# A DiT block's later modulation: four contraction tiles of 256 columns at a time in place of two of 512

## The chip, the cores and the metric

One core of a Trainium2 chip runs the whole block. The metric is the device time of one execution in microseconds (us). TensorE (PE) has a granted clock of 1.2 or 2.4 GHz; the profile gives it as a share of the higher one.

## The reference

A diffusion-transformer block: 1024 latent tokens and 256 context tokens of width 1024. From the conditioning vector c come six modulation rows, each 1024 long: shift, scale and gate of the mixer and of the experts.

```python
mod_l = (jax.nn.silu(c) @ w_ada[l] + b_ada[l])[:, None, :]
sh1_l, sc1_l, gt1_l, sh2_l, sc2_l, gt2_l = jnp.split(mod_l, 6, axis=-1)
u_c, u_l = hybrid_mixer(modulate(ctx, sh1_c, sc1_c), modulate(x, sh1_l, sc1_l), ...)
x = post_norm(DEEP_ALPHA * x + gt1_l * u_l, ln_g[l, 0], ln_b[l, 0])
f_l = hierarchical_moe(modulate(x, sh2_l, sc2_l).reshape(B * L, D), *moe_args)
x = post_norm(DEEP_ALPHA * x + gt2_l * f_l, ln_g[l, 1], ln_b[l, 1])
```

The mixer projects all tokens, runs a gated delta rule (four heads, two directions, with a triangular solve for each chunk of 64) and a gated linear recurrence, and projects back. The experts are 32 in four groups; each token goes to two.

## The kernel before

The work stands in stages, one after the other in time: the first two modulation rows, the layer norm and the transposition of the tokens (to about 85 us); the projections with everything that hangs on them (85 to some 556 us); the scan over chunks with the output projection, norms and router (to 850 us); the experts and the last norm (to the end).

The change is in the second stage. `proj_cm` (lines 407 to 414) loads 128 columns of `w_in` into a tile `wraw`, splits it into a high and a low part (`split_w`, lines 388 to 400: the high part on ScalarE or VectorE at line 398, the low part mostly on GpSimd at line 399), and runs three matmuls of each contraction tile (`mm3`, lines 402 to 405) into a PSUM tile `pj`. `head(h)` projects k, v and q of a head and convolves them (`conv`, line 434 on VectorE). `prep_a` makes decays, transposes (line 508) and products of the chunks (line 587); `prep_b` solves the triangular systems on VectorE, 31 steps of a product and a subtraction (lines 619 and 621). GpSimd works at `prep_a`'s masks (lines 518 and 552 to 557).

The other four modulation rows, 4096 channels, are computed in the gaps of that stage by `ada_late` (lines 688 to 715). It takes 512 channels at a time (loop over n, eight turns). For each, four loads on the SP queue (line 694) bring two contraction tiles of 128 rows by 512 columns each into `wraw`, a tag of three buffers that it shares with the loads of `w_in`. After each load stand two float32 matmuls (line 701): the stationary operand `cT[:, k, :]` is 32 columns wide, and the result goes to partitions 32g to 32g+31 of `pr`, with g = k % 4, so that it uses one strip of 32 columns of the array. The first four tiles open the four strips, the last four add to them. Then ScalarE copies `pr` (line 703), four matmuls of line 707 (eight records) sum the strips into four columns of a `pm` tile, and VectorE adds the bias (line 709). At the end the rows go to DRAM (line 715).

The tiles `pm` and `pj` have four PSUM buffers each (`PA['PM']`). `ada_late` is a generator: `next(side, None)` is called once after each piece of a head (lines 828 to 838), and each load and each copy ends in a yield. So the program's text sets only a priority. The order of the instructions on each engine is drawn up by the framework from its own estimates of durations (line 1649):

```python
with _tile.TileContext(nc, schedule_with_timeline_sim=True) as tc:
```

Engines then work their queues in order.

Of the kernel before, what the change touches and what calls it, by code (L numbers as in the profile page):

```python
# [9 lines left out]
F32 = mybir.dt.float32  # L10
# [8 lines left out]
P = 128  # L19
# [62 lines left out]
PA = {'ORD': 'x0 z1 x1 g0 z2 z0 x2 x3 g1 g2 g3 z3', 'ZB': 'qvsa', 'ADV1': 1, 'ADV2': 2, 'PER': 1, 'A0': 0, 'SQB': 1, 'GELU': 0, 'GSTG': 1, 'PM': (4, 4), 'HIV': (3, 8, 10, 14, 17, 20, 23), 'LOV': (2, 4, 21), 'C1V': (0, 1, 3, 4, 5, 14, 15, 19, 23), 'PSS': 0, 'TOK': (('kt', 4), ('v', 4)), 'EMV': 0, 'RGV': 0, 'CVB': 3, 'WRB': 3, 'HO': 'kvq', 'SQP': 0, 'YMA': 0}  # L82
# [5 lines left out]
def hybrid_block(ctx, tc, x, c, ctx_in, c_ctx, w_ada, b_ada, w_in, conv_qkv_w, dn_a_log, dn_dt_bias, dn_onorm_w,  # L88
         rg_conv_w, rg_conv_b, rg_wa, rg_ba, rg_wi, rg_bi, rg_lambda, w_out, ln_g, ln_b,
         router_wg, router_bg, router_we, router_be, w_e_gate, w_e_up, w_e_down, ranks, only, out):  # L90
    nc = tc.nc
# [20 lines left out]
    def pm():  # L112
        return psx[1].tile([P, 512], F32, name="pm", tag="pm", bufs=psx[2])

    def pj():
        return psx[1].tile([P, 512], F32, name="pj", tag="pj", bufs=psx[3])
# [65 lines left out]
    def later(s, after):  # L182

        tc.add_manual_dep(s.ins, after.ins.name, mybir.DependencyInfo(mybir.DependencyClass.Sync, mybir.DependencyReason.SCHED_ONLY), reason="needed sooner")
        return s
# [4 lines left out]
    cT = ca.tile([P, KT, 32], F32, name="cT")  # L190
# [3 lines left out]
    w_ada_v = w_ada[0].rearrange("(k p) n -> p k n", p=P)  # L194
# [71 lines left out]
    for gi, (tiles, t0) in enumerate((((8, 9), 1024), ((0, 1, 2, 3), 0), ((4, 5, 6, 7), 512))):  # L266
        nt = len(tiles)
        N = nt * P
        s = 0 if t0 < 1024 else 1
        pbd = pj()  # L270
        for k in range(KT):
# [10 lines left out]
            g = k % 4  # L282
# [94 lines left out]
    wp = wps.enter_context(tc.tile_pool(name="wp", bufs=1, side="right"))  # L377
# [310 lines left out]
    def ada_late():  # L688

        for n in range(8):  # L690
            pr = pj()
            for q in range(4):
                w = wp.tile([P, 2, 512], F32, name="wraw", tag="wraw", bufs=PA["WRB"])
                s = nc.sync.dma_start(w, w_ada_v[:, 2 * q:2 * q + 2, 2048 + n * 512:2560 + n * 512])
                if len(ada) < ADAN:
                    ada.append(later(s, lastx))
                yield
                for i in range(2):
                    k = 2 * q + i
                    g = k % 4  # L700
                    nc.tensor.matmul(pr[32 * g:32 * g + 32, :], cT[:, k, :], w[:, i, :], start=k < 4, stop=k >= 4)
            r = wp.tile([P, 512], F32, name="cv", tag="cv", bufs=PA["CVB"])
            nc.scalar.copy(r, pr)
            yield
            p1 = pm()
            for i in range(4):
                nc.tensor.matmul(p1[:, i:i + 1], r[:, i * P:(i + 1) * P], sel32[:, 0:1], start=True, stop=True)
            c0 = 4 * n
            nc.vector.tensor_tensor(mcol[:, c0:c0 + 4], p1[:, 0:4], bc_[:, 16 + c0:20 + c0], op=ALU.add)

        p1 = pm()
        nc.tensor.transpose(p1[0:32, 0:P], mcol, ident)
        r = wp.tile([P, 512], F32, name="cv", tag="cv", bufs=PA["CVB"])
        nc.scalar.copy(r[0:32, 0:P], p1[0:32, 0:P])
        nc.sync.dma_start(md[0].rearrange("(k p) -> k p", p=P), r[0:32, 0:P])
# [103 lines left out]
    def z_gate(h):  # L819
# [6 lines left out]
        nc.sync.dma_start(zd[:, h, :], zT)  # L826

    side = ada_late()
    rest_ = [dict(x=rg, z=z_gate, g=rg_out)[c_[0]](int(c_[1])) for c_ in PA["ORD"].split()]
    nu_ = 0  # L830
# [92 lines left out]
    w = {}  # L923
# [669 lines left out]
    for t0 in range(0, 8, 2):  # L1593
# [21 lines left out]
        for t in ts:  # L1615
# [6 lines left out]
            for b in range(2):  # L1622
                c0 = 64 * (t if (t + b) % 2 == 0 else 15 - t)
# [30 lines left out]
```

## Time and profile before

| what | value |
|---|---|
| median of three runs | 1289.57 us (1284.93 to 1298.79) |
| the profiled execution | 1280.62 us |
| its span, first to last instruction | 1278.9 us |
| mean granted clock of PE | 0.925 |
| PE busy | 1112.5 us (87%) |
| DVE busy | 682.3 us (53%) |
| ACT busy | 422.4 us (33%) |
| POOL busy | 424.9 us (33%) |

Engines: PE is TensorE's matmuls, PEld its weight loads, DVE VectorE, ACT ScalarE, POOL GpSimd, SP the queue that issues most DMAs. A busy time is the union of an engine's records; a matmul's record includes its way through the array, so records of neighbouring matmuls overlap, and the time that a matmul holds PE is read from start to start. A float32 matmul leaves two records. Names such as `pj<-wraw,cT` are out<-in by the program's tiles; `128*32 128x512` is 128 rows and 32 columns of the array, and 128 partitions by 512 elements of the moving operand. What stands in square brackets is the idle time of the engine before the instruction, and what ended it.

### The profile page before, as it was taken

The page shows a single profiled execution, that of the slowest core. Times are in us where ns is not written, and L with a number is a line of the kernel's source. Part 1 is how long each engine was busy: PE and PEld are TensorE (multiplying, and loading weights), DVE is VectorE, ACT ScalarE, POOL GpSimd, SP SyncE. Part 2 cuts the span into 40 slices and gives each one's busy share as a digit, 9 for nine tenths or more (in the row PEclk, how much of TensorE's full clock was granted, in tenths as well). Part 3 has the DMA queues.
Part 4 walks back from the last instruction along what each step waited for, and adds up shares of the span by engine and source line. Part 5 has one row for each costly group of instructions (what it writes and reads, how often), then busy time and mean ns, then how long its engine had stood idle before and what let it go on. Part 6 is the DMA issues. An engine that isn't in the chain of part 4 may idle for free.

```text
span 1278.9 us, 18429 instructions
## 1 busy us (share of the span) xinstructions
PE 1112.5 (87%) x6810; PEld 701.4 (55%) x6810; DVE 682.3 (53%) x1570; ACT 422.4 (33%) x755; POOL 424.9 (33%) x492
## 2 busy tenths in 40 slices
PE   4799998998999989987999999984898999999720
PEld 1357775776767677665667777772323433443210
DVE  3737479487684975875446766654211322222227
ACT  0535324233321727971222446540211212112003
POOL 1511414232242223353640176841211322222225
PEclk8799999999897999996999999975999999999975
DMA  9413453645536231009886255349999999999955
GB/s 335 163 49 93 140 149 94 189 139 140 141 111 160 69 104 37 17 19 306 266 256 214 93 188 185 114 186 332 336 332 355 342 309 307 308 311 315 314 178 169
DMA packets 208883, 251.43 MB, mean 197 GB/s; under 512 B 37276, under 2 KB 164440, under 8 KB 208792
## 3 DMA queue, kind: packets, MB, share of 16 engines
q1 hardware_dynamic: 194128, 215.94, 53.0%
q0 software_dynamic: 7888, 16.80, 5.7%
q10 hardware_dynamic: 6776, 17.50, 3.5%
q8 instruction: 54, 0.88, 0.3%
q14 instruction: 37, 0.30, 0.1%
HBM read 206.39 MB, written 55.20 MB: 205 GB/s over the span
## 4 chain that ended last, share of the span: by engine, by line
PE 39%; DMA 29%; DVE 17%; issue 6%; POOL 3%; SPq 3%; ACT 3%; DVEq 0%; POOLq 0%; ACTq 0%
DMA w<-in_w_e_up_dram 8%; DMA acc<-y,tbri 5%; PE pj L403 4%; PE pj L405 4%; PE pj L404 4%; DMA acc<-y,rows_to 4%; DMA d<-in_w_e_down_dram 4%; DVE s L621 4%; DVE s L619 4%; DMA wada<-in_w_ada_dram 2%; PE pu L1471 2%; PE p L1148 2%; PE pf L403 2%; PE pf L405 2%; PE pf L404 2%
## 5 line engine op out<-in xcount | busy, mean ns | idle before, releaser
L1471 PE MATMUL pu<-w,xT 128*32 128x512 f32 (+2 forms) x848 | 189.1, 614 | 19.0 <-DMA w<-in_w_e_up_dram 17.0
L403 PE MATMUL pj<-hhi,whi 128*128 128x512 f32 (+1 forms) x480 | 188.6, 393 | 4.5 <-ACT s L439 2.8
L404 PE MATMUL pj<-hlo,whi 128*128 128x512 f32 (+1 forms) x480 | 185.9, 387 | 0.0
L405 PE MATMUL pj<-hhi,wlo 128*128 128x512 f32 (+1 forms) x480 | 184.3, 385 | 0.0
L1471 PEld LDWEIGHTS pu<-w,xT 128*32 128x32 f32 (+2 forms) x848 | 61.8, 135 | 116.9 <-issue 104.0
L403 PEld LDWEIGHTS pj<-hhi,whi 128*128 128x128 f32 x480 | 92.5, 193 | 49.6 <-issue 18.6
L399 POOL TENSOR_TENSOR wlo<-wraw,whi 128x1024 fp32r<-128x1024 f32 x21 | 52.8, 2513 | 155.2 <-ACT whi L398 87.3
L405 PEld LDWEIGHTS pj<-hhi,wlo 128*128 128x128 f32 x480 | 92.7, 193 | 20.8 <-issue 5.7
L1492 PE MATMUL py<-d,hT 128*32 128x512 f32 (+2 forms) x424 | 101.0, 598 | 3.1 <-DMA d<-in_w_e_down_dram 2.1
L404 PEld LDWEIGHTS pj<-hlo,whi 128*128 128x128 f32 x480 | 92.8, 193 | 19.3 <-issue 5.3
L1474 DVE TENSOR_TENSOR hid<-hid,pu 128x256 f32<-128x256 f32 x24 | 10.0, 421 | 138.0 <-ACT hid L1473 138.0
L1496 POOL DMA_INDIRECT acc<-y,rows_to x28 | 41.3, 1476 | 116.4 <-DMA acc<-y,rows_to 51.0
L619 DVE TENSOR_TENSOR s<-s,s 80x31 f32<-80x31 f32 (+15 forms) x124 | 65.4, 527 | 14.4 <-DMA s<-ad 11.8
L434 DVE SCALAR_TENSOR_TENSOR cv<-pj,par,cv 128x504 f32<-128x504 f32 (+3 forms) x96 | 63.9, 668 | 11.3 <-ACT cv L422 10.3
L1493 DVE SCALAR_TENSOR_TENSOR y<-py,tbw,gt 128x512 f32<-128x512 f32 x48 | 35.7, 750 | 62.9 <-PE py L1492 52.8
L1462 ACT ACTIVATE xT<-pf,mod 128x128 f32<-128x128 f32 x96 | 37.8, 455 | 89.4 <-PE pf L1458 82.8
L1464 DVE TENSOR_SCALAR xT<-pf,mod 128x128 f32<-128x128 f32 x96 | 34.8, 405 | 59.4 <-ACT xT L1462 50.2
L1449 POOL DMA_INDIRECT xg<-h2d,tbri x24 | 25.4, 1060 | 117.4 <-PE pf L1458 69.8
L1492 PEld LDWEIGHTS py<-d,hT 128*32 128x32 f32 (+2 forms) x424 | 31.7, 131 | 57.3 <-issue 51.5
L621 DVE TENSOR_TENSOR s<-s,s 80x31 f32<-80x31 f32 (+15 forms) x124 | 61.9, 499 | 2.3
L1473 ACT ACTIVATE hid<-pu 128x256 f32<-128x256 f32 x24 | 9.1, 384 | 147.0 <-PE pu L1471 147.0
L403 PE MATMUL pf<-whi,yh 128*128 128x512 f32 x128 | 53.9, 421 | 1.9 <-DVE x L974 1.2
(483 smaller groups left out, 2123.1 us busy)
## 6 DMA issues: line engine op xcount, KB each, us to landing
w<-in_w_e_gate_dram SPq DMA_DIRECT2D x32, 1024.0 KB, 7.9
w<-in_w_e_up_dram SPq DMA_DIRECT2D x32, 1024.0 KB, 8.3
d<-in_w_e_down_dram SPq DMA_DIRECT2D x32, 1024.0 KB, 6.4
st<-sp SPq DMA_DIRECT2D x52, 384.0 KB, 5.2
wraw<-in_w_ada_dram SPq DMA_DIRECT2D x32, 512.0 KB, 4.6
wraw<-in_w_in_dram SPq DMA_DIRECT2D x24, 512.0 KB, 5.3
wada<-in_w_ada_dram SPq DMA_DIRECT2D x4, 2048.0 KB, 8.4
sp<-t SPq DMA_DIRECT2D x12, 512.0 KB, 4.6
```

Of the source, the lines that this page charges most:

```text
L399: (nc.vector if i in PA["LOV"] else nc.gpsimd).tensor_tensor(lo, raw, hi.bitcast(F32), op=ALU.subtract)
L403: nc.tensor.matmul(o, lh, rh, start=start, stop=False)
L404: nc.tensor.matmul(o, lh, rl, start=False, stop=False)
L405: nc.tensor.matmul(o, ll, rh, start=False, stop=stop)
L434: nc.vector.scalar_tensor_tensor(yo, xi, w(j), yo, op0=ALU.mult, op1=ALU.add)
L619: nc.vector.tensor_tensor(t_, sa[:, j + 1:32, j:j + 1].to_broadcast([80, n, j + 1]), T[:, j:j + 1, 0:j + 1].to_broadcast([80, n, j + 1]), ...
L621: nc.vector.tensor_tensor(T[:, j + 1:32, 0:j + 1], T[:, j + 1:32, 0:j + 1], t_, op=ALU.subtract)
L1462: nc.scalar.activation(self.xT[:, i, 0:u], pt[:, k * P:k * P + u], AF.Identity, bias=mod2[:, 0, i:i + 1], scale=mod2[:, 1, i:i + 1])
L1471: nc.tensor.matmul(pu[o:o + n, :], self.xT[:, k, o:o + n], ws[r][:, k, :], start=k == 0, stop=k == KT - 1)
L1492: nc.tensor.matmul(py[o:o + n, :], self.hT[:, f, o:o + n], ws[r][:, f, qs], start=f == 0, stop=f == 1)
L1493: nc.vector.scalar_tensor_tensor(y[0:u, qs], py[0:u, :], self.weights[0:u], gt2[0:u, qs], op0=ALU.mult, op1=ALU.mult)
L1496: nc.gpsimd.indirect_dma_start(out=acc, out_offset=bass.IndirectOffsetOnAxis(ap=to[0:o + n], axis=0), in_=y[0:o + n], in_offset=None, boun ...
```

## The change

A load brings four contraction tiles of 256 channels in place of two of 512, and its four matmuls go to four strips of the array, 256 columns each. Loads, their bytes, buffers and yields keep their number. The two halves of the channels follow each other: contraction tiles 0 to 3 and 4 to 7 of the first 256 channels, then of the second.

```diff
             for q in range(4):
-                w = wp.tile([P, 2, 512], F32, name="wraw", tag="wraw", bufs=PA["WRB"])
-                s = nc.sync.dma_start(w, w_ada_v[:, 2 * q:2 * q + 2, 2048 + n * 512:2560 + n * 512])
+
+                a, c0 = q % 2, q // 2 * 256
+                w = wp.tile([P, 4, 256], F32, name="wraw", tag="wraw", bufs=PA["WRB"])
+                s = nc.sync.dma_start(w, w_ada_v[:, 4 * a:4 * a + 4, 2048 + n * 512 + c0:2304 + n * 512 + c0])
                 if len(ada) < ADAN:
                     ada.append(later(s, lastx))
                 yield
-                for i in range(2):
-                    k = 2 * q + i
-                    g = k % 4
-                    nc.tensor.matmul(pr[32 * g:32 * g + 32, :], cT[:, k, :], w[:, i, :], start=k < 4, stop=k >= 4)
+                for g in range(4):
+                    nc.tensor.matmul(pr[32 * g:32 * g + 32, c0:c0 + 256], cT[:, 4 * a + g, :], w[:, g, :], start=a == 0, stop=a == 1)
```

## Rows read from the trace of the kernel before

**Rows 1.** The page, busy tenths in 40 slices of 32 us
```profile
PE   4799998998999989987999999984898999999720
```

**Rows 2.** Windows: length, busy us (x instructions), granted clock, DMA share, GB/s
```profile
core 0: us, PE busy (x) PEld busy (x) DVE busy (x) ACT busy (x) POOL busy (x), PEclk, DMA share, GB/s
219.00:225.00 6.00, 4.82 (x12) 2.17 (x12) 4.41 (x15) 4.19 (x6) 0.00 (x0) 0.50 0.27 65
85.00:420.00 335.00, 322.51 (x2188) 240.48 (x2187) 226.87 (x548) 112.85 (x178) 101.17 (x71) 0.94 0.49 136
```

**Rows 3.** Chain of waits from 85 to 420 us, shares by line
```profile
by line: PE pj L403 12.5%; PE pj L405 11.7%; PE pj L404 11.5%; DVE s L619 10.4%; DVE s L621 9.7%; PE pj L701 5.8%; DVE cv L434 5.3%; PE pm L587 3.9%; PE pm L658 2.8%; DMA wraw<-in_w_in_dram 2.6%; PE pm L643 2.1%; PE pm L497 1.9%; PE pm L508
```

**Rows 4.** The later modulation, line 701: durations ns min/median/max, first and last start us
```profile
L701 PE MATMUL pj<-wraw,cT x128: 592/617/1063, 89.1 to 417.0; 128*32 128x512 f32 x128
```

**Rows 5.** Windows of line 701 alone: PE and PEld busy us
```profile
85.00:420.00 335.00, 37.24 (x128) 4.98 (x128) 0.94 0.49 136
```

**Rows 6.** Timeline of PE, one load's two tiles: start us, us
```profile
126.12 1.05 PE L701 MATMUL pj<-wraw,cT 128*32 128x512 f32 x4
127.10 0.50 PE L403 MATMUL pj<-hhi,whi 128*128 128x512 f32 x1
```

**Rows 7.** Timeline of PE, two loads' four tiles together, and the projection behind
```profile
133.91 1.06 PE L701 MATMUL pj<-wraw,cT 128*32 128x512 f32 x8
134.91 0.39 PE L403 MATMUL pj<-hhi,whi 128*128 128x256 f32 x1
...
135.49 0.40 PE L404 MATMUL pj<-hlo,whi 128*128 128x512 f32 x1
135.72 0.28 PE L405 MATMUL pj<-hhi,wlo 128*128 128x256 f32 x1
135.84 0.27 PE L403 MATMUL pj<-hhi,whi 128*128 128x256 f32 x1
```

**Rows 8.** Timeline of PE, one load at the lower clock
```profile
222.50 1.92 PE L701 MATMUL pj<-wraw,cT 128*32 128x512 f32 x4
224.36 0.58 PE L403 MATMUL pj<-hhi,whi 128*128 128x256 f32 x1
```

**Rows 9.** Timeline of PEld, weight loads of four tiles
```profile
133.91 0.16 PEld L701 LDWEIGHTS pj<-wraw,cT 128*32 128x32 f32 x8 [0.36 <-issue]
```

**Rows 10.** Timeline of PE, a load's two tiles cut apart
```profile
342.35 1.04 PE L701 MATMUL pj<-wraw,cT 128*32 128x512 f32 x2
343.33 0.44 PE L508 MATMUL pm<-ident,kT 128*128 128x128 f32 x2
343.70 1.05 PE L701 MATMUL pj<-wraw,cT 128*32 128x512 f32 x2
```

**Rows 11.** The page, DMA issues: KB each, median us to landing
```profile
wraw<-in_w_ada_dram SPq DMA_DIRECT2D x32, 512.0 KB, 4.6
wraw<-in_w_in_dram SPq DMA_DIRECT2D x24, 512.0 KB, 5.3
```

**Rows 12.** Line 701, what ended its waits: us, times
```profile
  DMA wraw<-in_w_ada_dram: 0.4, 1
```

**Rows 13.** Timeline of DVE in a triangular solve
```profile
207.22 0.37 DVE L619 TENSOR_TENSOR s<-s,s 80x207 f32<-80x207 f32 x1
207.62 1.35 DVE L621 TENSOR_TENSOR s<-s,s 80x207 f32<-80x207 f32 x1
...
213.32 2.36 DVE L621 TENSOR_TENSOR s<-s,s 80x175 f32<-80x175 f32 x1
...
219.98 0.15 DVE L709 TENSOR_TENSOR mcol<-pm,bc__93 128x4 f32<-128x4 f32 x1
```

**Rows 14.** Timeline of POOL beside it, first and last of seven
```profile
207.48 1.26 POOL L554 TENSOR_TENSOR e<-e,nu 128x640 f32<-128x640 f32 x1 [4.85 <-ACT e L523]
...
216.77 1.61 POOL L557 TENSOR_TENSOR e<-e,m 128x640 f32<-128x640 f32 x1
```

**Rows 15.** Timeline of PE beside it
```profile
220.18 0.69 PE L508 MATMUL pm<-ident,vT 128*128 128x128 f32 x2 [6.25 <-DVE mcol L709]
```

## Prediction

> **What bounds the kernel now.** I read the slices of the page first: PE is 9 tenths busy or nearly so from the second to the fifteenth slice, and the edited loop lives there [rows 1]. The windows make it sharper: from 85 to 420 us PE works 322.5 of 335 us, DVE 226.9, and the DMA engines are busy half the time [rows 2]. So while the later modulation is computed, PE hardly rests. The chain of waits for the same stretch says what a shorter PE would meet: the projections (lines 403 to 405) are 36% of it, the triangular solves on DVE (lines 619 and 621) 20%, and the edited line 701 5.8%, which is 0.058 x 335 = 19.4 us [rows 3]. All of line 701 is 37.2 us of PE [rows 5]. So about half of its time is paid for by the end, and the other half runs beside a solve that ends no sooner. What comes behind is one chain: scan stage and experts start on what this stage leaves, so that I let a gain or a loss at 420 us reach the end undiminished.
>
> **The change part by part.** First PE. A float32 tile is two records, the passes of one matmul. A load of today has two tiles, on two neighbouring strips of 32 columns. At the full clock its four records start at 126.12, and the projection behind them at 127.10: 0.98 us [rows 6]. The four records span 1.05 us and the later pass is 0.592 us long [rows 4], so the second pass begins 0.45 us after the first. Where the planner happens to put two loads together, four tiles on four strips take 133.91 to 134.91, 1.00 us [rows 7]. That is the key row: the other two strips cost 0.02 us, so a load that fills all four with half the columns should cost half the streaming. Columns do scale: in the projection behind, a step of 512 columns takes 135.49 to 135.72, 0.23 us, and one of 256 takes 0.12 us [rows 7]. Two passes of 0.45 us become two of 0.23, which saves 0.43 us and leaves 0.55 us a load.
>
> Two passes of 0.45 us are 0.90 us, and 0.98 us pass before the projection resumes [rows 6], so some 0.1 us a load goes with the change of tile shape; I leave it in, since there are still 32 changes. The Trainium skill (TensorEngine Tiling (Array Packing), Key Properties) says that changing the tiling mode drains the engine; the trace agrees. By that rule a load can't fall to half of 0.98 us, and by the other reading, that all of it halves, the gain would be 0.49 us a load and not 0.43.
>
> Sum for PE: 32 loads x 0.43 = 13.8 us. Four loads run partly or wholly at half clock, as the one at 222.50, which takes 1.86 us to the projection behind [rows 8] where the granted clock is 0.50 [rows 2], the level of 1.2 GHz in place of 2.4, after PE had stood still [rows 15]; these save once more as much, 1.7 us. The two places where loads already run together lose their old advantage: the four tiles of rows 7 take 1.00 us today and two quads in a row 2 x 0.45 + 0.1 = 1.0, so nothing is saved there and 0.9 us goes off; the other place, three loads at 89 us, costs as much. 13.8 + 1.7 - 1.8 = 13.7, say 14 us of PE.
>
> There are twice as many weight loads. Eight of them, two passes of four tiles, take 0.16 us side by side [rows 9]; a first pass of 0.23 us covers them. Without that cover they would add up to 32 x 0.16 = 5 us; I take 0.
>
> The loads keep their number, bytes, buffers and queue, so SP issues what it issued and no queue is passed. Their pieces go from 2 KB to 1 KB. No row of this stretch has 1 KB pieces for a load of this size; those of the input projection have 512 B pieces and land in 5.3 us, those of 2 KB in 4.6 us [rows 11]. So between 0 and 0.7 us a load, 22 us if every load were waited for; or a gain of as little, if shorter pieces mix better with the other transfers. Line 701 waited for a load once, 0.4 us [rows 12], because three buffers let a load go out well ahead, so that I take 0. It costs what it is only where that lead is gone. No wait is added: both halves of a load's matmuls wait for one transfer, as before.
>
> Now what of 14 us reaches the end. With every engine's order as it is, the gain can't be above what leaves the present chain: 19.4 x 14 / 37.2 = 7.3 us, because the rest of that chain keeps its length. Below, it is 0, if at each place the solve running beside is as late as PE was. PE has 12.5 us of rest in 335, so the path of PE and the path of DVE end close together at most joins, and part of the 7.3 us will turn into waits for line 621. I take 5 us, nearer to the chain's row than to nothing.
>
> The order doesn't stay, though. It is drawn up by the framework from its own estimates of durations, and other tile sizes give it another plan for all five engines. What a shift can do shows at 207 to 220 us. The solve's 0.37 us step becomes 1.35 and 2.36 us [rows 13] exactly while seven POOL instructions stand back to back [rows 14]; the little addition of line 709 queues behind it on DVE until 219.98 and holds a PSUM buffer, and PE stands still for 6.25 us [rows 15] and then has half the clock for six more [rows 2]. The Trainium skill (SBUF — State Buffer, Who interferes with whom) says that a DVE instruction with two SBUF inputs contends with a GpSimd instruction that reads SBUF; these rows agree. Such a burst costs 6.25 + 6 / 2 = 9 us, more than my whole gain, and whether the new plan has none, one or three is not to be read from the old trace. I take one, as now.
>
> **Sum.** The profiled execution takes 1280.62 us, 1.7 over its span; 1280.6 - 5 = 1275.6. The median of the runs shown is 1289.57, 0.7% above the profiled one; scaled by that, 1284.5 us. A difference of under 1%, 12.9 us, is about what can't be told from none.
>
> **The rivals.**
> *All of PE's gain arrives.* The new plan fills the freed PE time with projections, so that 14 us go: 1266.6, by the runs' median 1275.4. For it: PE has no rest in this stretch [rows 2], and DVE a third of it. Against: the solves' 20% of the chain [rows 3].
> *The four are cut apart.* The planner puts something else between tiles of a load: today three of 32 pairs are cut, as at 342.35, and each half then costs 1.0 us alone [rows 10]. A quad cut once costs 2 x 0.55 = 1.1 us, more than today's pair; with all of them cut nothing is left, 1289.6. Against it: three in 32 is few.
> *Slower: more bursts of POOL on a solve.* Price 9 us a burst, as worked out. One more eats the 5 us and leaves 4 on the other side; from two more on it is over 1%: 1280.6 - 5 + 18 = 1293.6, by the median 1302.7. For it: POOL works 101 us and DVE 227 of these 335 [rows 2], so there is a lot to collide, and a PE that arrives earlier waits longer. Against: the wait of 6.25 us occurs once in the stretch, and a new plan may as well remove it.
>
> **How the numbers follow.** Forecast (0 to 7 us gained, 5 likeliest) 0.45; all of PE's gain 0.22; cut apart 0.10; slower 0.23. The forecast and the cut case lie within 1%, the full gain just beyond it, the slower case beyond it mostly: faster 0.24, same 0.56, slower 0.20. The range reaches a little past both outer cases, 1268 to 1304, as a burst removed or added on top of either would; the forecast's own, 0 to 7 us gained, is 1282 to 1290.
>
> **What would show it.** In the profile after, line 701 should have 256 records of 256 columns, at the full clock some 0.4 us long, start in fours, and be busy about 20 to 23 us in place of 37.2; each quad should stand 0.55 us before the next projection. Its waits for the load should stay near 0.4 us, and the load's landing between 4.6 and 5.3 us. The share of line 701 in the chain should fall to some 12 us, and waits for lines 619 and 621 grow. I am wrong if quads take 0.9 us or more (strips not side by side), if line 701 waits for its load by microseconds, or if PE's time falls as said and the end moves by over 1% either way, which would be the plan's doing and not the matmuls'.

## The result, and the profile after

| | before | after |
|---|---|---|
| median of 20 runs each | 1287.03 us | 1297.22 us |
| ratio, 95% interval | | 1.0077 [1.0057, 1.0098] |
| span of the profiled execution | 1278.9 us | 1297.3 us |
| mean granted clock of PE | 0.925 | 0.911 |

The kernel became slower by 0.8%, some 10 us, where the forecast was a small gain (1284.5 us). The two profiles differ by more than the medians do, 18.4 us; the stages below show where that comes from.

The edited line first. Durations of line 701 and what its engine waited for, in the kernel after:

```profile
L701 PE MATMUL pj<-wraw,cT x256: 379/403/637, 89.8 to 413.6; 128*32 128x256 f32 x128
...
its engine sat idle before it (us, times) until:
  issue: 6.9, 21
```

Windows of line 701 alone, after (PE and PEld busy us):

```profile
85.00:420.00 335.00, 23.81 (x256) 5.89 (x256) 0.92 0.49 136
```

There are 256 records where there were 128 [rows 4], 0.40 us long in the median, and no wait for a load is left of the one before [rows 12]. The line keeps PE busy for 23.81 us in place of 37.24 [rows 5]: 13.4 us less. (The trace of after gives no time to landing for the loads, so that sign of the prediction stays unread.) The timeline of PE, after, has a quad between projections:

```profile
137.83 0.64 PE L701 MATMUL pj<-wraw,cT 128*32 128x256 f32 x8
138.40 0.39 PE L403 MATMUL pj<-hhi,whi 128*128 128x256 f32 x1
...
150.82 0.62 PE L701 MATMUL pj<-wraw,cT 128*32 128x256 f32 x2
151.37 0.34 PE L587 MATMUL pm<-kT 128*64 128x64 f32 x4
...
154.57 0.63 PE L701 MATMUL pj<-wraw,cT 128*32 128x256 f32 x6
```

From 137.83 to the projection at 138.40 a quad takes 0.57 us; a pair took 0.98 [rows 6]. At 150.82 one is cut after its first matmul (two records) and goes on at 154.57; four of the 32 are cut so, as three pairs were [rows 10].

Now the stretch. Windows of all engines, after, in the columns of [rows 2]:

```profile
85.00:420.00 335.00, 316.66 (x2326) 248.49 (x2327) 228.56 (x550) 111.91 (x177) 101.68 (x71) 0.92 0.49 136
```

PE is busy for 5.9 us less in this window, not 13.4, and its granted clock fell from 0.94 to 0.92 [rows 2]: so it seems that part of the freed time came back as slower matmuls, though a window of fixed length doesn't hold quite the same work in both. (The chain that the profile of after follows back from its end has no piece between 85 and 420 us, so the answer to [rows 3] is read from an experiment.) The big wait of [rows 15] is there again at almost the same place, on the timeline of PE, after:

```profile
221.77 0.69 PE L508 MATMUL pm<-ident,vT 128*128 128x128 f32 x2 [6.20 <-DVE mcol L709]
```

Last, the order. Before and after have the same instructions but for two more matmuls at each of 32 places, and still the plan differs on every engine: taking the longest sequence that the two lists of the held kernels below share, 392 of PE's 4568 instructions stand elsewhere, 133 of 1547 on DVE, 44 of 720 on ACT, 24 of 570 on SP and 9 of 553 on POOL.

The stages, from the starts and ends of lines in each trace: projections from the end of the last line 283 to the end of the last line 814, then to the end of the last line 1057 (scan and router), then the experts. "Held" is explained below. The last column is the granted clock in the window from 85 to 420 us.

| kernel | ratio, 95% interval | projections | of it from first line 770 | scan | experts | clock |
|---|---|---|---|---|---|---|
| before | | 487.4 | 156.6 | 287.9 | 414.9 | 0.94 |
| before, order held | 1.0021 [0.999, 1.0052] | 490.4 | 159.7 | 290.9 | 420.9 | 0.94 |
| new tiles, old order | 1.0029 [1.0004, 1.0053] | 484.0 | 157.1 | 290.6 | 426.6 | 0.92 |
| old tiles, new order | 1.0041 [1.0007, 1.0074] | 493.6 | 161.2 | 288.0 | 428.9 | 0.94 |
| after | 1.0077 [1.0057, 1.0098] | 493.7 | 161.3 | 285.6 | 428.6 | 0.92 |
| after, order held | 1.0066 [1.0033, 1.0098] | 496.8 | 162.2 | 286.8 | 418.1 | 0.92 |

The experts' stage scatters by 14 us over these profiles, with no pattern, and the profile of before has the shortest one of all; so the 18 us between the two spans say little. The projections say more: they are 6.3 us longer in after than in before, and 6.4 us longer in the held copies of the two. Of the first, 4.7 us arise behind the first line 770 (the gates of the recurrence), and the scan stage gives 2 to 4 us back.

### The profile page after: what moved, and what is told of

Read it like the earlier page. It is cut to its first block, busy times and chain, and to the rows that moved or that the text cites. A ratio compares the mean times of both kernels' runs of the same rounds, so it can differ in the third digit from the quotient of the medians.

```text
span 1297.3 us, 18685 instructions
## 1 busy us (share of the span) xinstructions
PE 1109.5 (86%) x6938; PEld 707.9 (55%) x6938; DVE 689.8 (53%) x1570; ACT 426.2 (33%) x759; POOL 427.6 (33%) x492
## 4 chain that ended last, share of the span: by engine, by line
PE 21%; DMA 18%; DVE 4%; POOL 4%; issue 3%; ACT 1%; SPq 0%; DVEq 0%; POOLq 0%; ACTq 0%
DMA w<-in_w_e_up_dram 7%; PE pu L1471 7%; DMA d<-in_w_e_down_dram 3%; PE py L1492 3%; DMA acc<-y,tbri 2%; DMA acc<-y,rows_to 2%; PE p L1148 2%; PE pf L403 1%; PE pf L405 1%; PE pf L404 1%; DMA x<-in_x_dram 1%; PE p L1118 1%; DMA st<-sp 1%; PE p L1136 1%; DVE d L1610 1%
## 5 line engine op out<-in xcount | busy, mean ns | idle before, releaser
L1471 PE MATMUL pu<-w,xT 128*32 128x512 f32 (+2 forms) x848 | 194.4, 631 | 22.8 <-DMA w<-in_w_e_up_dram 20.7
L403 PE MATMUL pj<-hhi,whi 128*128 128x512 f32 (+1 forms) x480 | 191.7, 399 | 5.7 <-ACT s L439 4.9
L404 PEld LDWEIGHTS pj<-hlo,whi 128*128 128x128 f32 x480 | 94.6, 197 | 19.4 <-issue 4.8
```

The lines of the kernel that those rows point to most:

```text
L403: nc.tensor.matmul(o, lh, rh, start=start, stop=False)
L404: nc.tensor.matmul(o, lh, rl, start=False, stop=False)
L1471: nc.tensor.matmul(pu[o:o + n, :], self.xT[:, k, o:o + n], ws[r][:, k, :], start=k == 0, stop=k == KT - 1)
```

## The experiments

**Which half of the change: tiles or order.** The framework can be told to keep an order: each instruction of an engine is made to follow the one before it in a list, without a semaphore. The lists come from the finished before and after.

```diff
+def hold_order(nc, tc):
...
+            if last is not None:
+                tc.add_manual_dep(i, last, mybir.DependencyInfo(mybir.DependencyClass.NoSync, ...), reason="order")
+            last = i.name
...
         hybrid_block(tc, *args)
+        hold_order(nc, tc)
```

In `new_tiles_old_order` the loads and tiles are those of after, and each quad stands where its pair stood; in `old_tiles_new_order` it is the other way round. `before_order_held` and `after_order_held` hold a kernel to its own order, as controls.

> The changed kernel (loads of 4 x 256, quads of 256 columns) with every engine's instructions held in the order of the kernel before; a quad stands where the pair of the same load stood. Theory 'the plan': the edit itself gives PE back 13 us of line 701 and the end some of it, and only the new order of the instructions made the kernel slower; then this is faster than the kernel before by 2 to 8 us, ratio 0.994 to 0.998. Rival 'the edit': the 1 KB pieces, the narrower matmuls or PE arriving early cost more than they give; then it is slower, ratio 1.004 or more, although nothing is reordered.

> The kernel before (loads of 2 x 512, pairs of 512 columns) with every engine's instructions held in the order that the changed kernel got; a pair stands where its quad's first tile stood. Theory 'the plan': slower than the kernel before by what the change cost and the matmuls' gain on top, 12 to 18 us, ratio 1.009 to 1.014. Rival 'the edit': the order is worth nothing, ratio 0.997 to 1.003.

> Control: the kernel before, its own order held by the same device; engine by engine the same instructions with the same waits. If what separates the first held run (ratio 1.0029, though its projection stage ended 3 us sooner) is a cost of the edit, this gives 0.998 to 1.002, and an expert stage near the 415 us of the profile before. If the expert stage varies from program load to program load by itself, its expert stage lies anywhere from 415 to 429 us, and the ratio may differ from 1 by up to 0.4%. The projection stage (end of line 283 to end of line 814) should repeat its 487.4 us within 1.5 us either way.

> Control: the changed kernel, its own order held. Ratio within 1.004 to 1.010 as the unheld one, projection stage 493.7 us within 3 us either way (the kernel before and its held copy differ by 3.0 us in it).

The controls say how finely this can be read. Before in its own order: 1.0021, with 1 in its interval, and projections of 490.4 us, 3.0 more than in before where I had allowed 1.5. After in its own order: 1.0066, beside its own 1.0077, and projections 3.1 us longer. So two profiles of one program differ by 3 us in this stage, and whether holding an order costs something itself isn't shown.

Both crossed kernels missed what was expected of them. New tiles in the old order, 1.0029 [1.0004, 1.0053], are not faster than before (0.994 to 0.998 expected), and no better than the control: the tiles alone bring no gain that shows at the end, and cost little if anything. Old tiles in the new order, 1.0041 [1.0007, 1.0074], are well short of the 1.009 to 1.014 expected, and as a ratio not apart from the control, nor from the new tiles in the old order. Two things do separate the orders. With the new tiles, the interval in the old order ends at 1.0053, below after's, which begins at 1.0057 (the held copy of after overlaps both). And the projections take 484.0 to 490.4 us in the old order and 493.6 to 496.8 us in the new one, whichever the tiles. So the longer projections go with the order, not with the matmuls; for the whole time this is likely and not shown.

**Why 13 us of PE are worth so little.** With the old order held, the chain of waits from 85 to 420 us in `new_tiles_old_order` is:

```profile
by line: DVE s L619 12.9%; DVE s L621 12.2%; PE pj L403 7.0%; PE pj L405 7.0%; PE pj L404 6.6%; DVE cv L434 6.6%; DMA wraw<-in_w_in_dram 4.7%; issue 4.4%; DMA ad<-A 3.9%; DMA s<-ad 2.9%; SPq L610 2.3%; DVE kT L434 2.1%; PE pm L587 2.1%; DMA
```

The projections went from 36% to 21%, the solves (lines 619 and 621) from 20% to 25%, and transfers of the solves' data (`ad`, `s`) came in [rows 3]. In the control, `before_order_held`, the chain is much as it was (projections 38%, solves 16%, line 701 7.0%), so the projections' fall is more than the scatter of two profiles. Line 701 is gone from the listed part, so it has under 2.1%, 7 us. PE arrives earlier and meets what it doesn't set. The largest single loss is at the products of line 643 behind the last solve. Timeline of PE, before:

```profile
390.61 2.41 PE L643 MATMUL pm<-XT,A 32*32 32x32 f32 x80 [1.56 <-DVE XT L635]
```

the same in `new_tiles_old_order`:

```profile
386.36 3.91 PE L643 MATMUL pm<-XT,A 32*32 32x32 f32 x80 [5.92 <-DVE XT L635]
```

Until here PE had run some 8 us ahead of before, counted by matching instructions; it now waits 4.4 us longer, and the same 80 matmuls take 3.91 us in place of 2.41, because the granted clock is low after the wait. Behind it the lead is 3 us. The windows from 380 to 420 us have the clock behind the busy times: 0.83 before, and 0.74 in `new_tiles_old_order` (that row stands further below). Before:

```profile
380.00:420.00 40.00, 38.44 (x343) 28.37 (x342) 17.37 (x34) 8.51 (x13) 10.10 (x10) 0.83 0.62 165
```

`half_tiles` goes further in the same direction. It holds the old order and leaves out half of line 701's matmuls (the upper four contraction tiles), so the modulation and all routing behind it are others, and only the projections are compared.

```diff
-                for g in range(4):
+                for g in range(4 * (a == 0)):
...
-                                     start=a == 0, stop=a == 1)
+                                     start=True, stop=True)
```

> The kernel after with the old order held, which leaves out half of line 701's matmuls (the upper four contraction tiles, 64 of 128 matmuls), so the modulation behind it is not the reference's and the routing changes: only the projection stage, to the end of the last line 814, is compared. TensorE holds line 701 for 23 us in the kernel after, so some 11.5 us are left out. If TensorE's time is on the path for all of it: the stage falls from 484 to 487 us to 473 to 476. If the solves and the cold clock behind each wait set the pace, as with the 13 us that the change freed: 482 to 488.

The projections took 481.4 us, 0.6 below the range of the one theory and 5 above that of the other: of 10.3 us more that line 701 leaves free (its windows give 10.46 us against 20.71 in `new_tiles_old_order`), 2.6 arrive. At line 643 the wait is now 9.09 us, timeline of PE:

```profile
382.99 3.91 PE L643 MATMUL pm<-XT,A 32*32 32x32 f32 x80 [9.09 <-DVE XT L635]
```

So PE's time in line 701 is mostly not on the path once the solves are met: 13 us less gave a stage 3 to 6 us shorter, 10 more gave 3 more. Each of these sets one profile beside another, and two profiles of one program differ by 3 us in this stage; what they rule out is that all of the time arrives.

**Tiles and loads apart.** Both kernels keep the old order and put weights at wrong places, so that everything behind the modulation is not the reference's (the routing changes, and their totals of 1.0786 [1.0748, 1.0824] and 1.0487 [1.0446, 1.0528] are not comparable); the projections are.

```diff
+                s = nc.sync.dma_start(w.rearrange("p (i j) n -> p i (j n)", j=2), w_ada_v[:, 2 * q:2 * q + 2, 2048 + n * 512:2560 + n * 512])
```

(`old_order_tiles_alone`: quads from loads with the old pieces of 2 KB)

```diff
+                s = nc.sync.dma_start(w.rearrange("p i (j n) -> p (i j) n", j=2), w_ada_v[:, 4 * a:4 * a + 4, 2048 + n * 512 + c0:2304 + n * 512 + c0])
```

(`old_order_loads_alone`: pairs from loads with the new pieces of 1 KB)

> Order of the kernel before held; quads of 256 columns, but from the old loads of 2 KB pieces (the bytes of a load are read as four tiles, so the later modulation is computed from misplaced weights). If the matmuls alone bring the gain of the projection stage, it takes 483 to 485 us as with both edits (484.0). If the 1 KB pieces took part in it, it differs by over 2 us.

> Order of the kernel before held; loads of 1 KB pieces, but the old pairs of 512 columns (again from misplaced weights). If the pieces cost nothing, the projection stage takes 486 to 489 us (487.4 before) and line 701 waits for its load by about 0.4 us in all. If they are what eats the gain, it takes 490 us or more.

Projections: 486.9 us with quads alone, 485.1 with the new loads alone, beside 487.4 and 490.4 for before. Shorter pieces show no cost (the stage is even 1 us below the range expected); line 701 waited for a load 0.4 us, once, as before. The quads alone made the matmuls as short (20.27 us in the window), and the stage by no more than the two profiles of before differ. It was to be 483 to 485 us, and over 2 us off was to mean that the pieces take part; 2.9 us off is within that same 3 us, so this stays undecided. The clock is the telling column: 0.91 with the quads alone, 0.96 with pairs on the new loads. Over all eighteen profiles of this study that window has 0.94 to 0.96 with pairs (five profiles) and 0.91 to 0.93 with quads (thirteen), whichever the order. That it falls because PE waits more is argued from places like line 643; `half_tiles`, with still less work in line 701, has 0.92 as well.

**Is it any shift of the plan?** `before_one_step_later` and `after_one_step_later` start the later modulation one piece later; the framework then plans anew.

```diff
-PA = {... 'A0': 0, ...}
+PA = {... 'A0': 1, ...}
```

> The kernel before, with the later modulation begun one piece of a head later (A0 = 1). No instruction changes, only the plan. Theory 'the plan': orders of this kind scatter the time by several us either way, ratio between 0.99 and 1.015 and not 1.000. Rival 'the edit': within 0.2% of the kernel before.

> The changed kernel, begun one piece of a head later (A0 = 1). Theory 'the plan': the time moves by several us against the changed kernel's ratio of 1.0077, either way. Rival 'the edit': it stays at 1.006 to 1.010.

Before: 1.0117 [1.0066, 1.0168]; after: 1.0122 [1.0067, 1.0178], from four runs each. A shift that saves and adds no instruction costs the kernel before 1.2%, at least about as much as the whole edit, and with that plan the two tile shapes are alike. That after moved against its own 1.0077 isn't shown, since its interval has that value in it. The projections are 499.0 and 497.4 us.

**Which part of the new order.** The new order has four more loads of ScalarE's function table (55 against 51, 1.283 us each). `new_order_old_act` has the new order on all engines but ACT.

```diff
 hold_order, PE, DVE, SP, POOL: the list of after
-hold_order, ACT: the list of after
+hold_order, ACT: the list of before
```

> The changed kernel in its own order on PE, DVE, POOL and SP, but ScalarE in the order of the kernel before. Theory 'table loads': the new order makes ScalarE load its function table 55 times in place of 51, 1.28 us each, three of the four after 550 us where the recurrence's gates wait for ScalarE; without them the ratio falls from 1.0077 to 1.001 to 1.004 and the projection stage (end of line 283 to end of line 814) from 493.7 to 486 to 490 us. Rival 'the rest of the order': the loads are hidden and the stage stays at 492 us or more, ratio 1.006 or more.

It has 51 loads and 1.018 [1.0134, 1.0227]; projections 503.1 us, scan 301.6, slower than either theory had it. A mixture of two plans makes engines wait for each other, and this run can't tell what the table loads cost. The next two split the order in time, at the last quad of line 701 (some 416 us).

```diff
 old_order_then_new:  all engines, to the last line 701: list of before;  then: list of after
 new_order_then_old:  all engines, to the last line 701: list of after;   then: list of before
```

> The changed kernel, all engines in the order of the kernel before up to the last tile of the later modulation (some 416 us), then in the new order: 53 table loads. If the tail's order makes the loss, the projection stage takes 488 to 492 us and the ratio is 1.004 to 1.008; if the order of the first part makes it, 484 to 487 us and a ratio of 1.003 as in the old order.

> The reverse: the new order up to the last tile of the later modulation, then the old one; 53 table loads. If the tail's order makes the loss, the stage takes 484 to 488 us and the ratio is about 1.003; if the first part's, 490 us or more and 1.006 or more.

1.0057 [1.0024, 1.0089] and 1.0041 [1.001, 1.0071]: not separated as ratios. The projections are: 494.4 us with the new order in the tail, 487.7 with the old one there. From the first line 770 on, the tail in the old order takes 156.6 to 160.1 us in seven profiles (the two of before, those with the old order held throughout, and `new_order_then_old`), in the new one 161.2 to 162.8 in four. And one interval doesn't scatter at all: from the fifth to the sixth start of line 770 it is 14.9 us in each of the seven and 19.4 in each of the four.

What differs there is seen on DVE, before (timeline):

```profile
508.89 1.49 DVE L752 TENSOR_TENSOR A<-A,X 128x1280 f32<-128x1280 f32 x1 [1.28 <-ACT A L785]
510.30 0.48 DVE L434 SCALAR_TENSOR_TENSOR kT<-pj,par,kT 128x255 f32<-128x255 f32 x1
510.69 0.68 DVE L756 TENSOR_TENSOR_SCAN X<-t,A 128x256 f32<-128x256 f32 x1
512.01 1.13 DVE L434 SCALAR_TENSOR_TENSOR kT<-pj,par,kT 128x504 f32<-128x504 f32 x2 [0.64 <-ACT kT L427]
513.06 2.34 DVE L757 TENSOR_TENSOR_SCAN X<-t,X,A 128x1024 f32<-128x1024 f32 x1
515.32 0.71 DVE L434 SCALAR_TENSOR_TENSOR kT<-pj,par,kT 128x496 f32<-128x496 f32 x1
515.94 1.97 DVE L399 TENSOR_TENSOR wlo<-wraw,whi 128x1024 fp32r<-128x1024 f32 x1
```

and after:

```profile
512.33 1.49 DVE L752 TENSOR_TENSOR A<-A,X 128x1280 f32<-128x1280 f32 x1 [0.50 <-ACT A L785]
513.74 1.13 DVE L434 SCALAR_TENSOR_TENSOR kT<-pj,par,kT 128x255 f32<-128x255 f32 x2
515.63 1.22 DVE L399 TENSOR_TENSOR wlo<-wraw,whi 128x1024 fp32r<-128x1024 f32 x1 [0.77 <-ACT whi L398]
516.77 0.68 DVE L756 TENSOR_TENSOR_SCAN X<-t,A 128x256 f32<-128x256 f32 x1
517.37 0.72 DVE L434 SCALAR_TENSOR_TENSOR kT<-pj,par,kT 128x504 f32<-128x504 f32 x1
518.00 4.15 DVE L757 TENSOR_TENSOR_SCAN X<-t,X,A 128x1024 f32<-128x1024 f32 x1
```

In the new order the split of a weight (line 399) stands in front of the scan, waits there for ACT, and the long scan comes late enough to meet a product on POOL, which reads SBUF (after, timeline of POOL):

```profile
517.69 2.32 POOL L774 TENSOR_TENSOR XT<-t 128x1280 f32<-128x1280 f32 x1 [10.87 <-ACT t L770]
```

The scan takes 4.15 us beside it in place of 2.34. The Trainium skill (SBUF — State Buffer, Who interferes with whom) says that a DVE instruction with two SBUF inputs contends with a GpSimd instruction that reads SBUF; this pair agrees. ACT, after, then waits for the scan and has two more table loads, around line 812 (timeline of ACT):

```profile
522.25 0.69 ACT L766 ACTIVATE A<-pm,hb 128x512 f32<-128x512 f32 x1 [3.15 <-DVE X L757]
...
530.93 1.06 ACT L398 CAST whi<-wraw 128x1024 fp32r<-128x1024 f32 x1
532.01 1.28 ACT L812 ACT_TABLE_LOAD   x1
533.30 0.60 ACT L812 ACTIVATE cv<-pj 128x512 f32<-128x512 f32 x1
533.79 0.47 ACT L766 ACTIVATE A<-pm,hb 128x256 f32<-128x256 f32 x1
534.28 1.28 ACT L770 ACT_TABLE_LOAD   x1
535.58 1.46 ACT L770 ACTIVATE t<-A,sn 128x1280 f32<-128x1280 f32 x1
```

Four runs move these instructions one by one.

```diff
 DVE, new order (scan_first):  752 434 434 -[399] 756 434 757 434 +[399] 775
 DVE, old order (scan_last):   752 434 +[399] 756 434 434 757 434 -[399] 434
 ACT, new order (gelu_later):  766 398 -[812] 766 770 766 766 771 766 +[812] 812 766
 both_moved:                   scan_first and gelu_later
```

> The kernel after in its own new order on every engine, but with one VectorE instruction (wlo of line 399, 1.22 us) moved from before the gates' scan of the third channel block (lines 756 and 757) to behind it. If this instruction makes the tail late: the interval from the fifth to the sixth start of line 770 falls from 19.4 us to 15 to 17.5, the scan of line 757 there takes 2.35 us instead of 4.15, the projection stage falls from 494 to 497 us to 490 to 493, and the ratio from 1.007 to about 1.004. If the rest of the order makes it late: the interval stays at 18.5 us or more, the stage at 494 or more, the ratio at 1.006 to 1.009.

> The tiles of the kernel after with the old order held on every engine, but with the same VectorE instruction (wlo of line 399) moved in front of the gates' scan, where the new order has it. If it makes the tail late: the interval from the fifth to the sixth start of line 770 rises from 14.9 us to 17 to 19.5, the projection stage from 484 to 487 or more, and the ratio from 1.003 to about 1.006. If it does not: the interval stays under 16 us and the ratio within 1.001 to 1.005.

> The kernel after in its new order, with one ScalarE instruction moved: the evaluation of line 812 that stands between the gates' lines 766 and 770 (at 533.3 us in the profile of after, with a table load of 1.28 us before it and another behind it) goes behind line 771, directly in front of the next line 812, so that the two share a table. If these loads are on the gates' path: the stretch from the fifth to the sixth start of line 770 falls from 19.4 us by two loads and the 0.60 us evaluation, 3.2 us, to 16.2 (15.5 to 17), and the ratio from 1.007 to 1.003 to 1.006. If the stretch waits for something else: 18.5 us or more, ratio 1.006 or more. A slower end would mean that the buffer of line 812's input, kept longer, holds TensorE up.

> Both single moves in the new order: the split of line 399 behind the scan, and the evaluation of line 812 behind line 771. If the two explain the stretch: it falls from 19.4 to 15.1 us (14.5 to 16; the old order has 14.9), and the tail from the first start of line 770 to the end of line 814 from 161.3 to 157 us as in the old order (156.6). The ratio then lies at 1.000 to 1.005. If it stays over 17 us, or the tail over 160, the order's cost lies elsewhere as well.

| kernel | fifth to sixth line 770 | sixth to seventh | first line 770 to line 814 | projections | ratio, 95% interval |
|---|---|---|---|---|---|
| after | 19.4 | 12.6 | 161.3 | 493.7 | 1.0077 [1.0057, 1.0098] |
| scan_first | 18.3 | 12.6 | 160.3 | 494.5 | 1.0033 [1.0002, 1.0063] |
| gelu_later | 16.2 | 15.7 | 160.4 | 491.6 | 1.0093 [1.006, 1.0125] |
| both_moved | 15.1 | 15.7 | 158.9 | 490.2 | 1.0046 [1.0019, 1.0073] |
| old order | 14.9 | 14.1 | 157.1 | 484.0 | 1.0029 [1.0004, 1.0053] |
| scan_last | 16.9 | 14.1 | 159.2 | 492.8 | 1.0052 [1.002, 1.0084] |

The split alone is worth 1.1 us taken away and 2.0 us put in, less than I expected at both ends (15 to 17.5 and 17 to 19.5). The scan itself did become short again in `scan_first`, timeline of DVE:

```profile
518.53 2.34 DVE L757 TENSOR_TENSOR_SCAN X<-t,X,A 128x1024 f32<-128x1024 f32 x1
```

but the product, which now starts behind it, took 3.73 us in place of 2.32, timeline of POOL:

```profile
519.26 3.73 POOL L774 TENSOR_TENSOR XT<-t 128x1280 f32<-128x1280 f32 x1 [10.89 <-ACT t L770]
```

In these two profiles the one of the pair that starts later is the long one, so the move hands part of the loss from DVE to POOL. And the collision isn't needed for a loss: in `scan_last` the scan takes 2.35 us with no product beside it, and the 2.0 us come with the split, which waits 2.54 us for ACT in front of it. The evaluation of line 812 gives the expected 3.2 us to the tenth, and both together the 15.1 that the sum says. ACT in `both_moved` shows it:

```profile
529.37 1.06 ACT L398 CAST whi<-wraw 128x1024 fp32r<-128x1024 f32 x1
530.31 0.50 ACT L766 ACTIVATE A<-pm,hb 128x256 f32<-128x256 f32 x1
530.84 1.46 ACT L770 ACTIVATE t<-A,sn 128x1280 f32<-128x1280 f32 x1
...
535.18 1.28 ACT L812 ACT_TABLE_LOAD   x1
536.47 1.09 ACT L812 ACTIVATE cv<-pj 128x512 f32<-128x512 f32 x2
539.47 0.69 ACT L766 ACTIVATE A<-pm,hb 128x512 f32<-128x512 f32 x1 [1.91 <-DVE vT L757]
```

Two evaluations share one table load, and line 770 starts with no load in front. But the next interval then grows by 3.1 us, with a wait of 1.91 us for the next scan in it: of 4.3 us won, 2.4 are left at line 814. So the cause of the 4.5 us in this stretch is shown: about 3.2 us are the two table loads and the evaluation between them, and 1.1 to 2.0 us the place of the split. It is not all of the 10 us. As ratios, `both_moved` lies below after with intervals that overlap, and `gelu_later` alone missed its expectation altogether: it has less of the stretch and no faster end.

How far two runs of one order can part, one pair shows. `scan_last` and `new_tiles_old_order` have the same order up to 512 us, and yet the last tile of line 701 ends at 420.2 us in the one and at 414.1 in the other. Windows of `new_tiles_old_order`:

```profile
380.00:420.00 40.00, 34.08 (x318) 26.48 (x318) 20.31 (x37) 11.33 (x15) 12.43 (x11) 0.74 0.65 168
...
235.00:239.00 4.00, 4.00 (x111) 3.53 (x112) 1.35 (x3) 0.51 (x2) 0.19 (x1) 1.00 0.86 243
239.00:251.00 12.00, 11.95 (x170) 9.97 (x168) 6.56 (x16) 4.67 (x8) 6.85 (x6) 1.00 0.51 145
```

and of `scan_last`:

```profile
380.00:420.00 40.00, 31.07 (x316) 24.45 (x314) 16.32 (x38) 5.21 (x9) 9.22 (x10) 0.70 0.63 170
235.00:239.00 4.00, 3.42 (x95) 3.08 (x89) 2.92 (x7) 0.45 (x2) 2.21 (x1) 1.00 0.42 127
239.00:251.00 12.00, 12.00 (x97) 10.28 (x98) 4.66 (x12) 3.85 (x6) 4.81 (x6) 0.57 0.50 143
```

From 239 to 251 us PE is busy throughout in both, at a granted clock of 1.00 in one run and 0.57 in the other. What went before differs: at 235 us `scan_last` was 2.6 us ahead by matching instructions, and it waited twice for a solve, timeline of PE:

```profile
237.10 0.81 PE L658 MATMUL pm<-ym,X 32*32 32x32 f32 x20 [0.37 <-DVE ym L647]
238.13 0.81 PE L658 MATMUL pm<-X,ym 32*32 32x32 f32 x20 [0.22 <-DVE ym L647]
```

where the other run has no wait. Counted from `new_tiles_old_order`, it falls back by 3.5 us from 235 to 265 us, by 2 more to 300, and by 3 at 380 to 400. Whether the short waits set the low clock off is not shown: `half_tiles` waits 0.4 us at the same line and keeps 1.00. The Trainium skill (TensorE: Matmul & The Clock Gate, What's actually happening) says that the number of slow matmuls at a kernel's start varies from run to run of one kernel; the place here lies 240 us in, so these rows are no test of that.

## Why the prediction was wrong

By its steps:

- *PE saves 14 us.* Right: 13.4 in busy time. A quad was to take 0.55 us and takes 0.57; the cut ones were to stay few, and are four.
- *Weight loads at nothing, loads at nothing.* Right, the first as far as the quad's 0.57 us tells, the second by a run of its own: 485.1 us with 1 KB pieces beside 487.4 and 490.4.
- *"I take 5 us, nearer to the chain's row than to nothing."* Mis-sized. With the order held, the projections are 3 to 6 us shorter in one profile and 1 to 4 in the one with the quads alone, about what two profiles of one program differ by, and the end is not apart from the control's, 1.0029 [1.0004, 1.0053] against 1.0021 [0.999, 1.0052]. The bound of 7.3 us took line 701's share of the old chain and let the rest keep its length. It didn't: the solves rose to 25% of the chain, the wait at line 643 from 1.56 to 5.92 us, and the clock fell from 0.94 to 0.92 in the whole window. The prediction did name the wait for the solves; it gave no price to a clock that is low behind such a wait, as at line 643.
- *"Whether the new plan has none, one or three is not to be read from the old trace. I take one, as now."* This is the step that failed and turned the sign. I counted the plan's change as bursts on a solve and set it to zero. The burst is there once, 6.20 us at 221.77, just as now. But the plan has hundreds of other places, and one of them, in the gates at 512 to 536 us, outside the stretch that I looked at, costs 4.5 us. In the projections the new order takes 493.6 to 496.8 us where the old one takes 484.0 to 490.4, some 7 us more in the mean of three profiles each, above my whole forecast and in the other direction; as a ratio, `old_tiles_new_order` has 1.0041 [1.0007, 1.0074].
- *The slower rival* had the right kind, a DVE instruction made longer by POOL and an order that brings them together, and the wrong place and size: in the gates, taking the split from in front of the scan, which is then short again, gave back 1.1 us, and the larger part there is ScalarE's table loads, which the prediction doesn't name. No second burst came on a solve. The time it gave, 1302.7, is nearer to what was measured than the forecast's, by another way, which is luck.
- *Cut apart, and all of PE's gain arrives*: neither. The matmuls are together, and most of their gain stays beside the solves. By its own prices the first of these rivals was set a little low: with every quad cut, 32 x (1.1 - 0.98) = 4 us would have been lost, not nothing.

The prediction's last sentence has the right kind: PE's time fell as said, and the end moved, by 0.8% where the sentence asked for over 1%, and as far as the runs show by the plan's doing. The share of line 701 in the chain fell as well, further than the 12 us that it gave. What stays open is the rest of the 10 us, some 4 of them behind the projections, where profiles of one and the same program differ by as much, and whether `gelu_later` is slow by its order or by its runs.

## What to carry to other kernels

Where a framework draws up the order from estimated durations, price an edit twice: once with the order held, once for the new plan, and take the second as a spread, here about 0.4 to 1.2% for edits that change next to no work. A shorter instruction on the busiest engine was worth here only the distance to the next chain, less what a slower clock took back; look in the row of that wait how far the other engine is behind. Compare a stage with a held copy of the same kernel before you believe a few microseconds.

## What the runs showed of the hardware

- With quads in place of pairs the granted clock in the window from 85 to 420 us was 0.91 to 0.93 (thirteen profiles), with pairs 0.94 to 0.96 (five), in every order: less work for TensorE, at a lower clock. With half of the quads left out it was 0.92.
- Two kernels with one order up to 512 us had a clock of 1.00 and of 0.57 from 239 to 251 us, with PE busy in both; one fell back by 3.5 us around that place.
- Four float32 tiles on four strips of 32 columns pass in 0.57 us for 256 columns, two for 512 columns in 0.98.
- A scan of 1024 columns on VectorE took 2.34 us alone and 4.15 us beside a GpSimd product of 2.32 us that had started 0.31 us earlier; where the scan had started first, it took 2.34 us and the product 3.73 us.
- A change of ScalarE's table took 1.28 us, and the next evaluation began 1.30 us after the load's start (534.28 to 535.58). The Trainium skill (ScalarE activation tables: per-element evaluation and per-set limits, What a function is on this engine) puts two functions of different sets one load of 1283 ns apart; the rows agree.
